# Feed-forward matmuls of 512 columns: high and low activations side by side

## The chip, the cores and the metric

The kernel runs on one core of a Trainium2 chip. The metric is the device time of one execution in microseconds (us). TensorE multiplies: a weight load (LDWEIGHTS) puts 128x128 values in its array, a MATMUL streams columns past them and adds the result into PSUM, which has eight banks of 512 float32 values on each of 128 partitions. VectorE and ScalarE read PSUM and do the elementwise work, GpSimd does a few small things, SyncE issues the weight DMAs.

## The reference

Two transformer blocks for 256 tokens of width 1024, in float32. The first has feed forward, a mixer, feed forward and a per-layer gate; the second has a mixer, memory attention and feed forward. Only the three feed-forward stages are touched by the change:

```python
def swiglu(x, w_gate, w_up, w_down):
    return (jax.nn.silu(x @ w_gate) * (x @ w_up)) @ w_down
...
        f = swiglu(rms_norm(h, ffn1_pre_g[i]), ffn1_w_gate[i], ffn1_w_up[i], ffn1_w_down[i])
        h = h + 0.5 * rms_norm(f, ffn1_post_g[i])
...
        gate, up = jnp.split(hf @ w_ffn_in[l], 2, axis=-1)
        x = x + (jax.nn.silu(gate) * up) @ w_ffn_out[l]
    return rms_norm_2(x, norm_final)
```

The width inside is 2816, which is 22 chunks of 128; the width outside is 8 chunks.

## The kernel before

Features lie on partitions, the 256 tokens on the free dimension. To get float32 accuracy out of the fast type float32r, each operand is split in two: a high part (a cast) and a low part (the rest, a subtraction). A product is then three matmuls, written in `mm3` (L187 to L190): high weights with high activations, low weights with high activations, high weights with low activations. Every `mm` is one weight load and one matmul at L184.

Weights come as blocks [128, 128], eight of them in a unit of 512 KB, in the order in which TensorE takes them. `Stream.take` hands out a block and sees to what is ahead of it: SyncE's DMA into a `raw` buffer (five of them), ScalarE's cast to the high part `wh` (L90, seven buffers, five units ahead) and VectorE's subtraction for the low part `wl` (L101, six buffers, four units ahead).

The order of all instructions is written by hand: each engine runs its own in the order in which the code issues them. Small steps are put off with `after(n, fn)`, and each `tick()` lets one more stretch of work pass.

`ffn` (called three times) has two parts.

- Gate and up: for the first four chunks of 128 outputs all eight input chunks are walked together, in four PSUM banks. Chunks 4 to 21 come one by one: `proj` runs 8 blocks for the gate into one half of a bank and 8 for the up branch into the other, so one unit of weights is one half chunk. Then `evac` multiplies the bank by 1/rms (`z`, L414, VectorE), applies Silu (L415, ScalarE), and puts off the product (s1, L418, VectorE), the high part `aH` (s2, L421, ScalarE) and the low part `aL` (s3, L424, VectorE) by one, two and three ticks.
- Down: for each of 8 output chunks, 22 blocks run into one half of a bank. `on_chunk` takes it away: in stages one and two `post_chunk` (a square, L304, a scaled copy, L330, both on ScalarE, and an addition, L305, on VectorE), in stage three `last_chunk` (an addition to the stream, L1223, on VectorE, then the rest).

The `pm` pool has five PSUM banks for these products, `pa` three for the rest. The activations' parts are separate tiles: `xH`, `xL` [128, 8, 256] and `aH`, `aL` [128, 22, 256]. While stage one runs, eight chunks of the memory operand are prepared by `mem_prep_chunk` (L464 to L467).

The mixers' `first_group` makes the values with tokens on partitions. There the activations are the loaded operand and four blocks of weights are streamed, so its matmuls have 512 columns.

Of the kernel before, what the change touches and what calls it, by code (L numbers as in the profile page):

```python
# [49 lines left out]
class Stream:  # L50
    """Weight blocks [128, 128] in the order in which the tensor engine takes them."""
# [19 lines left out]
    def split_now(self, u, cuts=(UB,)):  # L71
        """Both parts of unit u, for the start, when nothing else is to be done."""
# [43 lines left out]
def columns(a):  # L116
    """A view of 256 tokens in the order of the grid's columns as one in the order of its rows."""
    return a.rearrange("p (c r) -> p r c", r=GR)


class Bank:
    def __init__(self, t):
        self.t = t
        self.started = False


class Net:
# [63 lines left out]

    def mm3t(self, b, out, x, w, stop=False):
        self.mm(b, out, x[0], w[0])
        self.mm(b, out, x[0], w[1])
        self.mm(b, out, x[1], w[0], stop=stop)

    def proj(self, b, sub, name, m, ks, x):
        """One chunk of 128 outputs, features on partitions."""
        for i, k in enumerate(ks):
            w = self.ws.take(name, k, m)  # L200
            self.mm3(b, b.t[:, sub], w, (x[0][:, k], x[1][:, k]), stop=i == len(ks) - 1)
# [5 lines left out]
    def setup(self):  # L207
# [3 lines left out]
        self.xH = b.tile([P, DC, T], F32R, name="xH")  # L211
        self.xL = b.tile([P, DC, T], F32R, name="xL")
# [54 lines left out]
    def bcast(self, r):  # L267
        """1 / rms on every partition, in PSUM."""
# [28 lines left out]
    def squares(self, acc, in_, first, scale=1.0):  # L297
        """acc += (scale * in_)^2, chunk by chunk."""
# [8 lines left out]
    def sq_pair(self, j):  # L307
        """Squares of the stream's chunks 2j and 2j + 1."""
# [15 lines left out]
    def post_chunk(self, c, src, gain, scale=1.0):  # L324
        """Chunk c of a branch that is normed before it joins the stream."""
        nc = self.nc
        if c == 0:
            self.acc = self.new_acc()
        self.squares(self.acc, src, c == 0, scale)
        nc.scalar.activation(out=self.fg[:, c], in_=src, func=AF.Copy, scale=gain(c))  # L330

    def join(self, gain, fills, scale=None):
        """h += normed branch; then the next norm's operands, chunk by chunk."""
# [7 lines left out]
        x = (self.xH, self.xL)  # L341
# [43 lines left out]
    def add_chunk(self, c, src, gain, x):  # L385
        """h += branch, with the next norm's operands."""
# [7 lines left out]
    def add_pair(self, j, src, gain, x):  # L394
        """h += branch for two chunks of one bank, with the next norm's operands."""
# [8 lines left out]
    def ffn(self, gate, up, down, on_chunk, nk=4):  # L404
        nc = self.nc
        x = (self.xH, self.xL)
        with self.tc.tile_pool(name="ffn", bufs=1, reuse_waits="tile") as fp:
            self.fp = fp
            aH = fp.tile([P, FC, T], F32R, name="aH")
            aL = fp.tile([P, FC, T], F32R, name="aL")  # L410

            def evac(m, b):
                z = fp.tile([P, 2, T], F32, tag="z", name="z", bufs=6)
                nc.vector.tensor_tensor(out=z, in0=b.t, in1=self.row(rs), op=ALU.mult)  # L414
# [16 lines left out]
            for k in range(DC):  # L431
                for m in range(nk):
                    for sub, (name, off) in enumerate((gate, up)):
                        w = self.ws.take(name, k, off + m)
                        self.mm3(bs[m], bs[m].t[:, sub], w, (x[0][:, k], x[1][:, k]), stop=k == DC - 1)
# [4 lines left out]
            for m in range(nk):  # L440
                evac(m, bs[m])
            for m in range(nk, FC):
                b = self.bank()
                for sub, (name, off) in enumerate((gate, up)):
                    self.proj(b, sub, name, off + m, range(DC), x)
                    if sub == 1:
                        evac(m, b)
                    self.tick()
            for c in range(DC):
                b = self.bank()  # L450
                for k in range(FC):
                    w = self.ws.take(down, k, c)
                    self.mm3(b, b.t[:, 0], w, (aH[:, k], aL[:, k]), stop=k == FC - 1)
                    if k % 8 == 4:
                        self.tick()
                on_chunk(c, b.t[:, 0])

# [21 lines left out]
    def mem_k_task(self, c):  # L479
        nc = self.nc  # L480
        b = self.bank()
        for k in range(DC):
            w = self.ws.take("w_mem_kv_2", k, c)
            self.mm3(b, b.t[:, 0], w, (self.mH[:, k], self.mL[:, k]), stop=k == DC - 1)
# [29 lines left out]
    def ple_task(self, j):  # L514
        nc = self.nc
        b = self.bank()
        for sub in range(2):
            for k in range(2):
                w = self.ws.take("ple_w_proj", k, 2 * j + sub)
                self.mm3(b, b.t[:, sub], w, (self.pH[:, k], self.pL[:, k]), stop=k == 1)  # L520
# [6 lines left out]
    def first_group(self, win, vc, qc, kc):  # L527
        """Values (tokens on partitions) and the first two chunks of queries and keys, input chunk by chunk."""
        x = (self.xH, self.xL)
        vb = [self.bank() for _ in range(2)]  # L530
        qb = [self.bank() for _ in range(2)]
        for k in range(DC):
# [5 lines left out]
            for i in range(2):  # L538
                for sub, off in enumerate((qc, kc)):
                    w = self.ws.take(win, k, off + i)  # L540
                    self.mm3(qb[i], qb[i].t[:, sub], w, (x[0][:, k], x[1][:, k]), stop=k == DC - 1)
# [6 lines left out]
    def pair_task(self, win, m0, m1, evac):  # L548
        """Two output chunks in one bank; a generator of half tasks."""
        x = (self.xH, self.xL)  # L550
# [17 lines left out]
    def clear_pads(self, qz, vz):  # L568
        """The halves of queries and values that belong to a pair's other head."""
# [25 lines left out]
    def merge(self, tile, na, nb, oa, ob, tg, x, tanh_now):  # L595
        """merged = sigmoid(ga) * branch a + sigmoid(gb) * branch b, split, into x."""
# [25 lines left out]
    def from_merged(self, name, m, on_chunk):  # L622
        bs = [self.bank() for _ in range(2)]
        for ks in (range(DC - 2), (DC - 2, DC - 1)):
            for c in range(4):
                for k in ks:
                    w = self.ws.take(name, k, c)
                    self.mm3(bs[c // 2], bs[c // 2].t[:, c % 2], w, (m[0][:, k], m[1][:, k]), stop=k == DC - 1)
# [13 lines left out]
    def mixer1(self, fills):  # L642
        nc, tc, d = self.nc, self.tc, self.d
        with tc.tile_pool(name="mix1", bufs=1, reuse_waits="tile") as mp:
# [9 lines left out]
            oH = mp.tile([P, 4, T], F32R, name="oH")  # L654
            oL = mp.tile([P, 4, T], F32R, name="oL")
            yH = mp.tile([P, 4, T], F32R, name="yH")
            yL = mp.tile([P, 4, T], F32R, name="yL")
# [78 lines left out]
            def pool_mm(g):  # L736
                b = self.flat_bank()
                w = self.ws.take("pool_w", g, 0)
                self.mm3(b, b.t[:, 0:T], w, (yH[:, g], yL[:, g]), stop=True)
# [82 lines left out]
            m = (self.xH, self.xL)  # L822
# [589 lines left out]
```

## Time and profile before

| | |
|---|---|
| time, median of 3 runs | 1041.7 us (1041.17 to 1041.95) |
| span of the profiled execution, first to last instruction | 1040.2 us |
| TensorE busy | 1030.7 us, 99% |
| VectorE busy | 709.6 us, 68% |
| ScalarE busy | 545.7 us, 52% |
| GpSimd busy | 44.0 us, 4% |
| matmuls recorded | 8606 |

A profile is one execution; each record has a start and a length, and PE is TensorE's matmuls, PEld its weight loads, DVE VectorE, ACT ScalarE. Records of matmuls overlap, since the next one starts before the last one's results are all in PSUM, and a matmul's end is modelled. The distance between two starts tells what one costs in a row.

### The profile page before, as it was taken

Reading aid. Unit: us, or ns where it says so; the run is one execution under the profiler, and the core shown is the slowest. Engines: PE = TensorE matmul, PEld = TensorE weight load, DVE = VectorE, ACT = ScalarE, POOL = GpSimd, SP = SyncE. Lnnn points to the kernel's source line nnn. Section 1 sums busy time; section 2 is a strip of 40 time slices with the busy share of each in tenths; the row PEclk is TensorE's granted clock in tenths of the full one; section 3 lists DMA queues with packets and bytes.
Section 4 is the critical chain, followed back from the end, with each engine's and each line's share of the span. In section 5 each row is a group of like instructions: output and inputs, shape, how many; then the busy total and the mean of one; then the engine's idle time right before and its main releaser. Section 6 shows DMA issues by size and latency. Waiting matters only on the chain.

```text
span 1040.2 us, 20720 instructions
## 1 busy us (share of the span) xinstructions
PE 1030.7 (99%) x8606; PEld 1022.6 (98%) x8606; DVE 709.6 (68%) x1062; ACT 545.7 (52%) x857; POOL 44.0 (4%) x73
## 2 busy tenths in 40 slices
PE   9999999999999999999999999999999999999997
PEld 8999999999999999999999999999999999999996
DVE  7777754587858677666447776886678677666642
ACT  7655544464644555454446565465556555544431
POOL 0100000120000110000000111000001000000000
PEclk9999999999999999999999999999999999999999
DMA  8765564555545655556555666454566346555541
GB/s 287 244 214 181 194 215 171 181 190 185 194 151 166 229 179 193 184 191 190 196 167 177 195 201 194 159 168 157 160 222 226 110 139 219 187 199 182 178 147 42
DMA packets 55023, 191.50 MB, mean 184 GB/s; under 512 B 6400, under 2 KB 7936, under 8 KB 54928
## 3 DMA queue, kind: packets, MB, share of 16 engines
q1 hardware_dynamic: 52992, 184.37, 53.6%
q0 software_dynamic: 1936, 5.80, 1.8%
q8 instruction: 67, 1.10, 0.4%
q14 instruction: 28, 0.23, 0.1%
HBM read 187.00 MB, written 3.15 MB: 183 GB/s over the span
## 4 chain that ended last, share of the span: by engine, by line
PE 81%; issue 16%; DMA 1%; DVE 1%; SPq 0%; POOL 0%; POOLq 0%; DVEq 0%; ACT 0%
PE mm L184 77%; PE at L184 3%; DMA raw<-ws 1%; PE at L839 1%; DMA hg<-gx 0%; DVE sqp L315 0%; POOL r L264 0%; DVE wl L79 0%; SPq L63 0%; DVE wl L101 0%; DVE xL L290 0%; DVE fg L1323 0%; POOLq L1405 0%; DVEq L1405 0%; ACT wh L78 0%
## 5 line engine op out<-in xcount | busy, mean ns | idle before, releaser
L184 PE MATMUL mm<-xH,wh 128*128 128x256 f32 x1760 | 494.9, 281 | 0.0
L184 PE MATMUL mm<-xH,wl 128*128 128x256 f32 x1760 | 492.2, 280 | 0.8 <-DVE wl L79 0.4
L184 PE MATMUL mm<-xL,wh 128*128 128x256 f32 x1760 | 491.4, 279 | 0.0
L101 DVE TENSOR_TENSOR wl<-raw,wh 128x1024 fp32r<-128x1024 f32 x340 | 405.8, 1218 | 22.0 <-ACT wh L90 7.4
L90 ACT CAST wh<-raw 128x1024 fp32r<-128x1024 f32 x340 | 350.2, 1046 | 53.0 <-PE mm L184 33.5
L184 PEld LDWEIGHTS mm<-xH,wl 128*128 128x128 f32 x1760 | 331.2, 188 | 2.6 <-DVE wl L79 1.4
L184 PEld LDWEIGHTS mm<-xH,wh 128*128 128x128 f32 x1760 | 331.3, 188 | 1.6 <-ACT wh L78 0.8
L184 PEld LDWEIGHTS mm<-xL,wh 128*128 128x128 f32 x1760 | 331.1, 188 | 0.0
L184 PE MATMUL mm<-aH,wh 128*128 128x256 f32 x528 | 148.9, 282 | 0.0
L184 PE MATMUL mm<-aL,wh 128*128 128x256 f32 x528 | 148.2, 281 | 0.0
L184 PE MATMUL mm<-aH,wl 128*128 128x256 f32 x528 | 148.2, 281 | 0.0
L415 ACT ACTIVATE z<-z 128x256 f32<-128x256 f32 x66 | 27.2, 418 | 145.6 <-DVE z L414 145.5
L184 PEld LDWEIGHTS mm<-aH,wl 128*128 128x128 f32 x528 | 99.6, 189 | 0.0
L184 PEld LDWEIGHTS mm<-aH,wh 128*128 128x128 f32 x528 | 99.6, 189 | 0.0
L184 PEld LDWEIGHTS mm<-aL,wh 128*128 128x128 f32 x528 | 99.5, 189 | 0.0
L414 DVE TENSOR_TENSOR z<-mm,rs 128x512 f32<-128x512 f32 x66 | 44.7, 689 | 77.5 <-PE mm L184 71.8
L305 DVE TENSOR_TENSOR acc<-acc,sq 128x256 f32<-128x256 f32 x27 | 11.5, 425 | 65.0 <-ACT sq L304 64.9
L264 POOL TENSOR_TENSOR r<-v,mhalf 128x2 f32<-128x2 f32 x13 | 17.6, 1355 | 685.7 <-DVE v L262 685.7
L286 ACT ACTIVATE xH<-hg 128x256 fp32r<-128x256 f32 x48 | 23.6, 543 | 31.9 <-DVE hg L355 22.0
L304 ACT ACTIVATE sq<-mm 128x256 f32<-128x256 f32 x21 | 8.2, 390 | 53.8 <-PE mm L184 53.8
L418 DVE TENSOR_TENSOR z<-z 128x256 f32<-128x256 f32 x66 | 27.2, 423 | 8.7 <-ACT z L415 7.5
L424 DVE TENSOR_TENSOR aL<-z,aH 128x256 fp32r<-128x256 f32 x66 | 26.6, 415 | 0.0
(238 smaller groups left out, 1225.9 us busy)
## 6 DMA issues: line engine op xcount, KB each, us to landing
raw<-ws SPq DMA_DIRECT2D x340, 512.0 KB, 4.1
raw<-ws SPq DMA_DIRECT2D x9, 256.0 KB, 6.0
ub<-ub SPq DMA_DIRECT2D x8, 160.0 KB, 2.9
mraw<-memT POOLq DMA_DIRECT2D x8, 128.0 KB, 3.7
kd<-kv POOLq DMA_DIRECT2D x8, 128.0 KB, 3.0
vd<-kv POOLq DMA_DIRECT2D x4, 256.0 KB, 3.4
kv<-kd POOLq DMA_DIRECT2D x4, 256.0 KB, 6.2
kv<-vd POOLq DMA_DIRECT2D x4, 256.0 KB, 7.1
```

The lines of the kernel that those rows point to most:

```text
L90: self.nc.scalar.copy(out=h, in_=self.R[self.nhigh])
L101: self.nc.vector.tensor_tensor(out=l, in0=self.R.pop(u), in1=self.H[u].bitcast(F32), op=ALU.subtract)
L184: self.nc.tensor.matmul(out, lhsT, rhs, start=not b.started, stop=stop, skip_group_check=True)
L264: nc.gpsimd.tensor_tensor(out=r, in0=v, in1=self.mhalf, op=ALU.pow)
L286: self.nc.scalar.activation(out=self.ordered(x[0][:, c]), in_=self.rows(self.h[:, c]), func=AF.Copy, scale=gain(c))
L304: nc.scalar.activation(out=s, in_=in_, func=AF.Square, scale=scale)
L305: nc.vector.tensor_tensor(out=acc, in0=acc, in1=s, op=ALU.add)
L414: nc.vector.tensor_tensor(out=z, in0=b.t, in1=self.row(rs), op=ALU.mult)
L415: nc.scalar.activation(out=z[:, 0], in_=z[:, 0], func=AF.Silu)
L418: nc.vector.tensor_tensor(out=z[:, 0], in0=z[:, 0], in1=z[:, 1], op=ALU.mult)
L424: nc.vector.tensor_tensor(out=aL[:, m], in0=z[:, 0], in1=aH[:, m].bitcast(F32), op=ALU.subtract)
L839: self.nc.tensor.transpose(b.t[:, i * T + t * P:i * T + (t + 1) * P], u[:, t, kt * P:(kt + 1) * P], self.ident)
```

## The change

In the three feed-forward stages the product of a block is written with two matmuls, by a new `mm2`: the high weights meet high and low activations in one matmul of 512 columns, which fills both halves of a bank, and the low weights meet the high activations in one of 256, which is added to the first half. The two halves are summed at eviction. So that 512 columns lie side by side, every pair of high and low tiles becomes one tile [128, chunks, 2, 256] (class `Split`), also outside the feed-forward stages, where only the way of naming the parts changes. The first four chunks of gate and up, the last chunk of down, and all other stages keep `mm3`.

```diff
+class Split:
+    def __getitem__(self, i):
+        return self.t[:, :, i]
+    def at(self, k):
+        return self.t[:, k, 0], self.t[:, k, 1], self.t[:, k]
...
+    def mm2(self, b, w, x, stop=False):
+        self.mm(b, b.t, w[0], x[2])
+        self.mm(b, b.t[:, 0], w[1], x[0], stop=stop)
+
+    def wide(self, b, name, m, ks, x):
+        for i, k in enumerate(ks):
+            self.mm2(b, self.ws.take(name, k, m), x.at(k), stop=i == len(ks) - 1)
...
-        self.xH = b.tile([P, DC, T], F32R, name="xH")
-        self.xL = b.tile([P, DC, T], F32R, name="xL")
+        self.x = Split(b.tile([P, DC, 2, T], F32R, name="x"))
...
+        if more is not None:
+            nc.scalar.copy(out=self.fg[:, c], in_=more)
+            nc.vector.tensor_tensor(out=self.fg[:, c], in0=src, in1=self.fg[:, c], op=ALU.add)
+            src = self.fg[:, c]
...
-            aH = fp.tile([P, FC, T], F32R, name="aH")
-            aL = fp.tile([P, FC, T], F32R, name="aL")
...
+            a = Split(fp.tile([P, FC, 2, T], F32R, name="a"))
+            aH, aL = a[0], a[1]
...
+            def join2(z, b):
+                nc.scalar.copy(out=z, in_=b.t[:, 1])
+                nc.vector.tensor_tensor(out=z, in0=b.t[:, 0], in1=z, op=ALU.add)
...
             for m in range(nk, FC):
-                b = self.bank()
+                z = zt()
                 for sub, (name, off) in enumerate((gate, up)):
-                    self.proj(b, sub, name, off + m, range(DC), x)
+                    b = self.bank()
+                    self.wide(b, name, off + m, range(DC), x)
+                    join2(z[:, sub], b)
                     if sub == 1:
-                        evac(m, b)
+                        evac(m, z, z)
                     self.tick()
             for c in range(DC):
                 b = self.bank()
+                two = c < DC - 1
                 for k in range(FC):
                     w = self.ws.take(down, k, c)
-                    self.mm3(b, b.t[:, 0], w, (aH[:, k], aL[:, k]), stop=k == FC - 1)
+                    if two:
+                        self.mm2(b, w, a.at(k), stop=k == FC - 1)
+                    else:
+                        self.mm3(b, b.t[:, 0], w, a.at(k), stop=k == FC - 1)
                     if k % 8 == 4:
                         self.tick()
-                on_chunk(c, b.t[:, 0])
+                on_chunk(c, b.t[:, 0], b.t[:, 1] if two else None)
...
         nc.vector.tensor_tensor(out=h[:, c], in0=src, in1=h[:, c], op=ALU.add)
+        if more is not None:
+            nc.vector.tensor_tensor(out=h[:, c], in0=more, in1=h[:, c], op=ALU.add)
```

What stands in a row on VectorE in the gate and up part of stage one, before. The number behind a name is that of the buffer, so `mm_680` is a bank; in square brackets are the semaphores that an instruction waits for.

```order
L101 TENSOR_TENSOR wl_685<-raw_537,wh_641 128x1024 [waits DMAHW5_49]
L101 TENSOR_TENSOR wl_716<-raw_572,wh_683 128x1024 [waits DMAHW6_49,Activation_49]
L414 TENSOR_TENSOR z_742<-mm_680,rs_446 128x512 [waits PE_49]
L424 TENSOR_TENSOR aL_189<-z_669,aH_188 128x256 [waits Activation_49]
L418 TENSOR_TENSOR z_742<-z_742 128x256 [waits Activation_49]
L101 TENSOR_TENSOR wl_752<-raw_608,wh_714 128x1024 [waits DMAHW7_49]
```

The same place on VectorE after the change.

```order
L101 TENSOR_TENSOR wl_650<-raw_524,wh_612 128x1024 [waits DMAHW5_49]
L443 TENSOR_TENSOR z_644<-mm_645,z_644 128x256 [waits Activation_49]
L101 TENSOR_TENSOR wl_676<-raw_554,wh_648 128x1024 [waits DMAHW6_49]
L443 TENSOR_TENSOR z_644<-mm_671,z_644 128x256 [waits Activation_49]
L446 TENSOR_TENSOR z_644<-z_644,rs_443 128x512 [waits DVE_49]
L456 TENSOR_TENSOR a_186<-z_582,a_186 128x256
L450 TENSOR_TENSOR z_644<-z_644 128x256 [waits Activation_49]
L101 TENSOR_TENSOR wl_706<-raw_584,wh_674 128x1024 [waits DMAHW7_49]
```

Two additions (L443) have come in, one after each half chunk, and the first of them stands between two weight splits that followed each other before; the z multiplication reads the sum and no longer the bank.

ScalarE at the same place, before:

```order
L421 CAST aH_188<-z_528 128x256 [waits DVE_49]
L90 CAST wh_574<-raw_464 128x1024 [waits DMAHW3_49,PE_49,Activation_49]
L415 ACTIVATE z_602<-z_602 128x256 [waits DVE_49]
L90 CAST wh_610<-raw_498 128x1024 [waits DMAHW4_49,PE_49,Activation_49]
L421 CAST aH_188<-z_602 128x256 [waits DVE_49]
L90 CAST wh_641<-raw_537 128x1024 [waits DMAHW5_49,PE_49,Activation_49]
```

And after:

```order
L90 CAST wh_648<-raw_554 128x1024 [waits DMAHW6_49]
L442 COPY z_644<-mm_645 128x256 [waits PE_49,Activation_49]
L453 CAST a_186<-z_582 128x256 [waits DVE_49]
L90 CAST wh_674<-raw_584 128x1024 [waits DMAHW7_49]
L442 COPY z_644<-mm_671 128x256 [waits PE_49]
L447 ACTIVATE z_644<-z_644 128x256 [waits DVE_49]
L90 CAST wh_704<-raw_610 128x1024 [waits DMAHW0_49]
```

A copy out of the bank (L442) that waits for TensorE now stands behind each weight cast.

## Rows read from the trace of the kernel before

**Rows 1.** The page, part 1: busy time, share, instructions of each engine.

```profile
PE 1030.7 (99%) x8606; PEld 1022.6 (98%) x8606; DVE 709.6 (68%) x1062; ACT 545.7 (52%) x857; POOL 44.0 (4%) x73
```

**Rows 2.** The cores: span and mean granted TensorE clock.

```profile
core 0: 1040.2 us, clock 0.998
```

**Rows 3.** TensorE's waits: who waited for whom, total us, times, longest us.

```profile
PE at L230 <- DVE fg L227: 1.2, 1, 1.2
PE at L184 <- ACT sq L1235: 1.0, 1, 1.0
PE mm L184 <- DVE wl L79: 0.4, 2, 0.2
PE mm L184 <- DVE wl L101: 0.3, 1, 0.3
```

**Rows 4.** Groups by shape: line, engine, out<-in, shape, count | busy us, mean ns | idle.

```profile
L184 PE MATMUL mm<-xL,wh 128*128 128x256 f32 x1760 | 491.4, 279 | 0.0
L184 PE MATMUL mm<-wh,xL 128*128 128x512 f32 x32 | 12.7, 397 | 0.0
L184 PEld LDWEIGHTS mm<-xL,wh 128*128 128x128 f32 x1760 | 331.1, 188 | 0.0
```

**Rows 5.** Timeline of VectorE, gate and up, stage two: start us, length us [idle before].

```profile
431.73 0.69 DVE L414 TENSOR_TENSOR z<-mm,rs 128x512 f32<-128x512 f32 x1 [1.73 <-PE mm L184]
432.33 0.41 DVE L424 TENSOR_TENSOR aL<-z,aH 128x256 fp32r<-128x256 f32 x1
432.90 0.42 DVE L418 TENSOR_TENSOR z<-z 128x256 f32<-128x256 f32 x1 [0.16 <-ACT z L415]
433.25 2.35 DVE L101 TENSOR_TENSOR wl<-raw,wh 128x1024 fp32r<-128x1024 f32 x2
437.33 0.69 DVE L414 TENSOR_TENSOR z<-mm,rs 128x512 f32<-128x512 f32 x1 [1.73 <-PE mm L184]
```

**Rows 6.** Timeline of TensorE in the first mixer's first group: start us, length us.

```profile
207.05 0.40 PE L184 MATMUL mm<-wh,xH 128*128 128x512 f32 x1
...
208.21 0.40 PE L184 MATMUL mm<-wh,xL 128*128 128x512 f32 x1
208.45 0.28 PE L184 MATMUL mm<-xH,wh 128*128 128x256 f32 x1
...
209.85 0.39 PE L184 MATMUL mm<-wh,xH 128*128 128x512 f32 x1
...
221.05 0.39 PE L184 MATMUL mm<-wh,xH 128*128 128x512 f32 x1
```

**Rows 7.** Groups by shape: an addition out of PSUM, a copy out of PSUM.

```profile
L1223 DVE TENSOR_TENSOR hg<-mm,hg 128x256 f32<-128x256 f32 x8 | 3.4, 425 | 31.8 <-PE mm L184 31.8
L276 ACT COPY rs<-at 128x256 f32<-128x256 f32 x6 | 2.2, 372 | 17.4 <-PE at L184 17.4
```

**Rows 8.** Timeline of VectorE in stage one, a pair with memory preparation.

```profile
64.28 0.69 DVE L414 TENSOR_TENSOR z<-mm,rs 128x512 f32<-128x512 f32 x1 [1.73 <-PE mm L184]
65.86 0.48 DVE L466 SCALAR_TENSOR_TENSOR mL<-mraw,hg,mH 128x256 fp32r<-128x256 f32 x1 [0.89 <-ACT mH L465]
...
69.88 0.69 DVE L414 TENSOR_TENSOR z<-mm,rs 128x512 f32<-128x512 f32 x1 [0.26 <-PE mm L184]
```

**Rows 9.** Timeline at the end: the last product and its addition.

```profile
1031.46 0.29 PE L184 MATMUL mm<-aL,wh 128*128 128x256 f32 x1
1031.79 0.42 DVE L1223 TENSOR_TENSOR hg<-mm,hg 128x256 f32<-128x256 f32 x1 [7.12 <-PE mm L184]
```

**Rows 10.** Timeline of TensorE: first matmul of down in stage one, first after it.

```profile
132.17 0.28 PE L184 MATMUL mm<-aH,wh 128*128 128x256 f32 x1
...
194.83 0.28 PE L184 MATMUL mm<-mH,wh 128*128 128x256 f32 x1
```

**Rows 11.** Timeline of TensorE: first mixer's branch products and what follows them.

```profile
308.61 0.28 PE L184 MATMUL mm<-yH,wl 128*128 128x256 f32 x1
...
331.53 0.28 PE L184 MATMUL mm<-xH,wh 128*128 128x256 f32 x1
```

More of the change, by code (lines that the diff above doesn't have):

```diff
@@ L200, in proj @@
             w = self.ws.take(name, k, m)
-            self.mm3(b, b.t[:, sub], w, (x[0][:, k], x[1][:, k]), stop=i == len(ks) - 1)
+            self.mm3(b, b.t[:, sub], w, x.at(k), stop=i == len(ks) - 1)
     def row(self, t):
@@ L322, in new_acc, with post_chunk @@
         return self.tmp.tile([P, T], F32, tag="acc", name="acc", bufs=2)
-    def post_chunk(self, c, src, gain, scale=1.0):
+    def post_chunk(self, c, src, gain, scale=1.0, more=None):
         nc = self.nc
@@ L483, in mem_k_task @@
             w = self.ws.take("w_mem_kv_2", k, c)
-            self.mm3(b, b.t[:, 0], w, (self.mH[:, k], self.mL[:, k]), stop=k == DC - 1)
+            self.mm3(b, b.t[:, 0], w, self.m.at(k), stop=k == DC - 1)
             if k < DC - 1:
@@ L519, in ple_task @@
                 w = self.ws.take("ple_w_proj", k, 2 * j + sub)
-                self.mm3(b, b.t[:, sub], w, (self.pH[:, k], self.pL[:, k]), stop=k == 1)
+                self.mm3(b, b.t[:, sub], w, self.p.at(k), stop=k == 1)
                 if 2 * sub + k < 3:
@@ L540, in first_group @@
                     w = self.ws.take(win, k, off + i)
-                    self.mm3(qb[i], qb[i].t[:, sub], w, (x[0][:, k], x[1][:, k]), stop=k == DC - 1)
+                    self.mm3(qb[i], qb[i].t[:, sub], w, x.at(k), stop=k == DC - 1)
             if k == DC - 2:
@@ L653, in mixer1 @@
             tg2 = mp.tile([P, 4, 2, T], F32, name="tg2")
[L654 to L657, printed above, removed]
+            o = Split(mp.tile([P, 4, 2, T], F32R, name="o"))
+            y = Split(mp.tile([P, 4, 2, T], F32R, name="y"))
+            oH, oL, yH, yL = o[0], o[1], y[0], y[1]
             tg1 = self.fg.rearrange("p (a b) t -> p a b t", b=2)
@@ L738, in pool_mm @@
                 w = self.ws.take("pool_w", g, 0)
-                self.mm3(b, b.t[:, 0:T], w, (yH[:, g], yL[:, g]), stop=True)
+                self.mm3(b, b.t[:, 0:T], w, y.at(g), stop=True)
                 sc = self.gv[:, G_SCALE + g:G_SCALE + g + 1]
@@ L1151, in trans @@
                 b = self.transposed(st[h])
-                pH, pL = (mp.tile([P, 2, T], F32R, tag="p" + i, name="p" + i, bufs=n) for i, n in (("H", 2), ("L", 1)))
+                p = Split(mp.tile([P, 2, 2, T], F32R, tag="p", name="p", bufs=2))
+                pH, pL = p[0], p[1]
                 bt = b.t.rearrange("p (a t) -> p a t", a=2)
@@ L1217, in memory, with last_chunk @@
             outk((6, 7), True)
-    def last_chunk(self, c, src):
+    def last_chunk(self, c, src, more):
         nc = self.nc
```

79 lines of the change are left out of this document (41 added, 38 removed).

## The prediction

> **What bounds the kernel now.** The page's busy shares come first [rows 1]: TensorE has work in 99% of the span, VectorE in 68%, ScalarE in 52%. The view of the cores [rows 2] gives a mean granted clock of 0.998, so TensorE stands at its 2.4 GHz level nearly all the time. The view of TensorE's waits comes next [rows 3]: it waited 1.2 us for the set-up, 1.0 us at the very end and 0.7 us for weight parts in 1040.2 us. So no engine feeds TensorE too slowly, and the time is the sum of what its instructions cost in a row. An edit can gain only by making those cheaper, and can lose by making them dearer or by letting something late enough to stop them.
>
> A busy share does not say what one instruction costs. The groups by shape [rows 4] give 280 ns for a matmul of 256 columns, about 400 ns for one of 512 and 188 ns for a weight load, but the records overlap, so these are lengths and not prices. The price is the distance from start to start. In the gate and up part VectorE's evictions mark it: the start of one z multiplication to the next is 437.33 - 431.73 = 5.60 us [rows 5], and between them TensorE runs 2 x 8 blocks of three matmuls, 48 in all. That is 116.7 ns for 256 columns, or 350 ns for a block. The clock alone would allow 256/2.4 = 106.7 ns. The question is whether the missing 10 ns belong to the instruction or to the columns.
>
> **The change on TensorE.** Each block of weights used three matmuls of 256 columns (high x high, low x high, high x low). Now it uses one of 512 (high weights against both parts of the activations) and one of 256. The columns stay 768; one matmul and one weight load go. Counting from the loops: 18 chunks x 2 x 8 = 288 blocks in the gate and up part, 7 x 22 = 154 in the down part, three feed-forward stages, so 3 x 442 = 1326 instructions go.
>
> Their price can be read in the first mixer, where the values are already made by matmuls of 512 columns [rows 6]. One step there is six matmuls of 512 and twelve of 256, 18 instructions and 6144 columns. Five steps take 221.05 - 207.05 = 14.00 us, 2.800 us each. Twenty-four matmuls of 256, the same columns in 24 instructions, take 24 x 116.7 = 2.800 us in the gate and up part. Six instructions fewer save nothing. Inside a step, six of 512 take 208.45 - 207.05 = 1.40 us and twelve of 256 take 209.85 - 208.45 = 1.40 us: the time goes with the columns, 0.456 ns each. The rows are good to 0.01 us; on 5.60 us that is 5 ns for 24 matmuls, so a fixed cost above 0.8 ns per instruction would show. TensorE's term is therefore 1326 x 0, within plus or minus 1326 x 0.8 ns = 1.1 us. I take 0, the middle, because the two quotients are equal.
>
> The Trainium skill says otherwise: "TensorE: Matmul & The Clock Gate", section "Back-to-back issue gap", gives N/2.4 + 2.5 ns from start to start, so a fixed 2.5 ns per matmul; by it the sum would be 1326 x 2.5 = 3.3 us less, an estimate. Its 109 ns for 256 columns and 216 for 512 are below the 116.7 and 233 of these rows, and the step of 2.800 us does not show its fixed part. The page "Perfetto Trace Analysis", section "Identifying the Most-Contended Engine", judges TensorE by the busy share of its weight loads, which here is 98% of the span; taken at its word it speaks for the change, which takes a third of the loads away in these stages. The rows differ: with one load for 512 columns the pace is what it is with one load for 256.
>
> **The change on the evictions.** The two sums of a block chain now stand in the two halves of a bank. In gate and up each half chunk gets a ScalarE copy of one half and a VectorE addition of the other, 36 of each per stage. In down the first seven chunks of stages one and two get the same pair, and those of stage three one more addition. None of these existed; the nearest rows are an addition out of PSUM of this shape, 425 ns, and a ScalarE copy out of PSUM, 372 ns [rows 7]. For the whole kernel that is 129 additions more on VectorE (55 us) and 122 copies on ScalarE (45 us), all beside TensorE as long as it never waits for them.
>
> Does it? The pair of half chunks shown is the test. In 5.60 us VectorE now runs z, the low part aL, the product, and two weight splits from 431.73 to 435.60, and then idles 1.73 us until TensorE has finished the next pair [rows 5]. After the change two additions (0.85 us) come in, and once a pair VectorE stands for the ScalarE copy that its addition needs (0.4 us). 1.73 - 0.85 - 0.4 leaves about 0.5 us idle: VectorE still ends ahead of TensorE. The order also moves one of the two weight splits behind the other half chunk's addition, so it now waits for TensorE's first half chunk; it splits a unit needed four units (11.2 us) later, so nobody notices 2.8 us. In stage one eight pairs also carry the memory's preparation: there the waits are 0.89 and 0.26 us [rows 8], 1.15 us against 1.25 us of new work, a pair that ends 0.1 us late, and the next pair has 0.5 us to catch up. ScalarE's queue gets two copies (0.75 us) between weight casts that have a lead of five units; what is queued behind a waiting copy is the next cast, and it has 14 us.
>
> A bank now holds half a chunk, not a whole one, and is free only after the addition, some 0.8 us after its last matmul. TensorE takes a new bank every 2.8 us and five rotate, so a bank is wanted again some 11 us after it was finished. In down a matmul now needs both parts of an activation chunk at its start; the last low part is issued at block 12 of the first 22 and wanted at block 21, 9 x 0.35 = 3.1 us later, with one split (1.2 us) and itself (0.4 us) to do. Cost 0; without that cover it would be at most 1 us in each stage. The last chunk of down keeps the old form, so the tail after the final matmul (1031.46 to the end [rows 9]) and the two joins start as before: 0.
>
> **The sum.** 0 on TensorE (-1.1 to +1.1), 0 on the evictions, 0 at the seams: a span of 1040.2 us again. The runs had a median of 1041.7, 1.5 us above that span, which does not change: I forecast **1041.5**, between 1040.4 and 1043.
>
> **Rivals.**
> (A) There is a fixed cost per matmul after all, which shows when 512 and 256 alternate at every instruction. The before trace alternates only in runs of six and twelve. For it: 10 ns per matmul are unexplained by the clock. Against it: the step of 2.800 us includes a change each way. At three times the resolution of the rows, 2.4 ns, it gives 1326 x 2.4 ns = 3.2 us: **1038.5**. Chance 0.12. The rule of "TensorE: Matmul & The Clock Gate" in the Trainium skill would end there too.
> (B) The down part speeds up. From the first matmul on a to the first that follows it, 528 take 194.83 - 132.17 = 62.66 us [rows 10], 118.7 ns each and not 116.7. If that extra 2 ns comes from where the high and low parts lie or from the weight loads, it may go: 462 blocks x 3 x 2 ns = 2.8 us, **1038.9**. Against it: a keeps its place and size, only the parts are interleaved. Chance 0.13; with some other gain, 0.02.
> (C) The slower side: the pace depends on which tile is streamed, and the re-laid tiles fall on a slow one. The mixer's branch products stream other tiles, and 191 matmuls there take 331.53 - 308.61 = 22.92 us [rows 11], 120.0 ns each at the same clock. If every merged block went at this pace, gate and up would lose 864 x 3 x 3.3 ns = 8.6 us and down 462 x 3 x 1.3 ns = 1.8 us: **1052**. If gate and up only fell to the pace of down, 864 x 3 x 2 ns = 5.2 us, **1046.7**. It decides from 0.5 ns per 256 columns on. Against it: x is at 116.7 in this stage and keeps its place. Chance 0.05 for the full price, 0.07 for the smaller.
> (D) VectorE becomes the bound in gate and up. It needs more than 5.60 us of work in a pair, 0.5 us over my count. At 1 us over, 18 pairs fall 18 us behind, 11 of them covered by the lead: 7 us in each stage, **1062**. Chance 0.03.
>
> **How the numbers follow.** The forecast has 0.58; A 0.12, B 0.13, other gains 0.02; C 0.12; D 0.03. A measurement here tells about 0.2% (2.1 us) from no change, so faster 0.27, same 0.58, slower 0.15. The range 1037.8 to 1047 leaves out A and B together, the full C and D, some 0.15.
>
> **What would show it.** Right: z to z in gate and up again about 5.60 us, starts 0.233 and 0.117 us apart in alternation; TensorE's matmul count down by 1326 and its share still 99%; VectorE idle some 0.5 us in a pair. A: a pair of 512 and 256 below 0.348 us. B: the down part of a stage below 61.8 us. C: a pair above 0.352 us in gate and up. D: TensorE waiting for the wl splits or for the L443 additions. I would be wrong if one merged pair differs from 0.350 us by more than 2 ns.

## The result, and the profile after

The changed kernel takes 1034.9 us (median, 1034.7 to 1035.3); the kernel before, measured beside it, 1041.8 us (1041.2 to 1042.5). The ratio is 0.9935, 95% interval 0.9921 to 0.9949: 7 us faster, below the forecast of 1040.4 to 1043 and below its wider range from 1037.8 on. The span fell from 1040.2 to 1032.9 us at the same mean granted clock, 0.998.

The page's first part, busy time of each engine (beside [rows 1]):

```profile
PE 1023.2 (99%) x7280; PEld 961.8 (93%) x7280; DVE 758.4 (73%) x1191; ACT 585.2 (57%) x979; POOL 44.0 (4%) x73
```

8606 - 7280 = 1326 matmuls are gone, as counted; VectorE and ScalarE have the new work (129 and 122 instructions more). TensorE is at 99% as before, so the gain is not idle time that was filled. TensorE's waits say the same (who waited for whom, total us, times, longest us); they are those of [rows 3] within 0.1 us:

```profile
PE at L252 <- DVE fg L249: 1.2, 1, 1.2
PE at L197 <- ACT sq L1275: 1.0, 1, 1.0
PE mm L197 <- DVE wl L101: 0.4, 1, 0.4
PE mm L197 <- DVE wl L79: 0.4, 2, 0.2
```

So the matmuls themselves became cheaper. Where, the starts at the borders of the feed-forward stages tell. Timeline of TensorE in the changed kernel, first matmul of down and first matmul after it in stages one and two, first and last of down in stage three (start us, length us):

```profile
130.97 0.40 PE L197 MATMUL mm<-a,wh 128*128 128x512 f32 x1
...
192.11 0.28 PE L197 MATMUL mm<-m,wh 128*128 128x256 f32 x1
...
483.87 0.40 PE L197 MATMUL mm<-a,wh 128*128 128x512 f32 x1
...
545.01 0.28 PE L197 MATMUL mm<-p,wh 128*128 128x256 f32 x1
...
961.10 0.40 PE L197 MATMUL mm<-a,wh 128*128 128x512 f32 x1
...
1024.16 0.28 PE L197 MATMUL mm<-a,wh 128*128 128x256 f32 x1
```

In the kernel before, those of stage one are [rows 10], the last is in [rows 9], and the other three are these:

```profile
487.52 0.28 PE L184 MATMUL mm<-aH,wh 128*128 128x256 f32 x1
...
550.18 0.28 PE L184 MATMUL mm<-pH,wh 128*128 128x256 f32 x1
...
967.24 0.28 PE L184 MATMUL mm<-aH,wh 128*128 128x256 f32 x1
```

| stretch | before, us | after, us | gained, us |
|---|---|---|---|
| start to the end of gate and up, stage one | 132.17 | 130.97 | 1.20 |
| down, stage one | 62.66 | 61.14 | 1.52 |
| to the end of gate and up, stage two | 292.69 | 291.76 | 0.93 |
| down, stage two | 62.66 | 61.14 | 1.52 |
| to the end of gate and up, stage three | 417.06 | 416.09 | 0.97 |
| down, stage three | 64.22 | 63.06 | 1.16 |

Down gained 4.2 us and the rest 3.1 us, of the 7.3 us of the span. Each stretch that holds 288 merged blocks of gate and up is about 1 us shorter. The mixers and the memory attention, where nothing was merged, gave nothing that shows.

What one merged pair costs is read in gate and up, stage two. Timeline of TensorE:

```profile
431.17 0.39 PE L197 MATMUL mm<-x,wh 128*128 128x512 f32 x1
431.40 0.28 PE L197 MATMUL mm<-x,wl 128*128 128x256 f32 x1
431.52 0.39 PE L197 MATMUL mm<-x,wh 128*128 128x512 f32 x1
...
433.25 0.39 PE L197 MATMUL mm<-x,wh 128*128 128x512 f32 x1
```

From 431.17 to 433.25 there are six pairs: 2.08 us, 346.7 ns each, where three matmuls of 256 took 350.0. In down of stages one and two the mean of 176 blocks is 347.4 ns (61.14 us / 176), with the 22 blocks of the last chunk in it, which kept three matmuls; the merged pairs alone go at 346.7 ns there too, where three matmuls took 356.0 (62.66 us / 176 blocks). 864 x 3.3 ns = 2.9 us in gate and up and the 4.2 us of down make 7.1 of the 7.3 us; the rest lies in stage one, whose 1.20 us are more than 288 x 3.3 ns = 0.96 us.

VectorE in one pair of half chunks of the same stage, beside [rows 5] (start us, length us [idle before]):

```profile
429.46 0.69 DVE L446 TENSOR_TENSOR z<-z,rs 128x512 f32<-128x512 f32 x1
430.07 0.42 DVE L456 TENSOR_TENSOR a<-z,a 128x256 fp32r<-128x256 f32 x1
430.64 0.43 DVE L450 TENSOR_TENSOR z<-z 128x256 f32<-128x256 f32 x1 [0.15 <-ACT z L447]
430.98 1.22 DVE L101 TENSOR_TENSOR wl<-raw,wh 128x1024 fp32r<-128x1024 f32 x1
432.12 0.42 DVE L443 TENSOR_TENSOR z<-mm,z 128x256 f32<-128x256 f32 x1
432.45 1.22 DVE L101 TENSOR_TENSOR wl<-raw,wh 128x1024 fp32r<-128x1024 f32 x1
434.55 0.42 DVE L443 TENSOR_TENSOR z<-mm,z 128x256 f32<-128x256 f32 x1 [0.88 <-ACT z L442]
435.01 0.69 DVE L446 TENSOR_TENSOR z<-z,rs 128x512 f32<-128x512 f32 x1
```

z to z is 435.01 - 429.46 = 5.55 us, against 5.60. The two additions L443 are there, and VectorE still stands for 0.88 us until TensorE has finished the next half chunk and ScalarE has copied it.

### The profile page after: what moved, and what is told of

Read it like the earlier page. It is cut to its first block, busy times and chain, and to the rows that moved or that the text cites. A ratio compares the mean times of both kernels' runs of the same rounds, so it can differ in the third digit from the quotient of the medians.

```text
span 1032.9 us, 18212 instructions
## 1 busy us (share of the span) xinstructions
PE 1023.2 (99%) x7280; PEld 961.8 (93%) x7280; DVE 758.4 (73%) x1191; ACT 585.2 (57%) x979; POOL 44.0 (4%) x73
## 4 chain that ended last, share of the span: by engine, by line
PE 81%; issue 16%; DMA 1%; DVE 1%; SPq 0%; POOL 0%; POOLq 0%; DVEq 0%; ACT 0%
PE mm L197 77%; PE at L197 3%; DMA raw<-ws 1%; PE at L876 1%; DMA hg<-gx 0%; DVE sqp L337 0%; POOL r L286 0%; DVE wl L79 0%; SPq L63 0%; DVE wl L101 0%; DVE x L312 0%; DVE fg L1363 0%; POOLq L1445 0%; DVEq L1445 0%; ACT wh L78 0%
## 5 line engine op out<-in xcount | busy, mean ns | idle before, releaser
L197 PE MATMUL mm<-x,wh 128*128 128x256 f32 (+1 forms) x2784 | 650.3, 315 | 0.1
L197 PE MATMUL mm<-x,wl 128*128 128x256 f32 x1824 | 512.3, 281 | 0.9 <-DVE wl L101 0.4
L197 PEld LDWEIGHTS mm<-x,wh 128*128 128x128 f32 x2784 | 459.5, 188 | 35.5 <-ACT wh L78 1.0
L197 PEld LDWEIGHTS mm<-x,wl 128*128 128x128 f32 x1824 | 343.8, 189 | 2.7 <-DVE wl L79 1.2
L197 PE MATMUL mm<-a,wh 128*128 128x512 f32 (+1 forms) x594 | 185.2, 368 | 0.0
L197 PE MATMUL mm<-a,wl 128*128 128x256 f32 x528 | 147.5, 280 | 0.0
L197 PEld LDWEIGHTS mm<-a,wh 128*128 128x128 f32 x594 | 107.2, 188 | 19.1
L197 PEld LDWEIGHTS mm<-a,wl 128*128 128x128 f32 x528 | 99.2, 188 | 0.0
L443 DVE TENSOR_TENSOR z<-mm,z 128x256 f32<-128x256 f32 x108 | 45.3, 420 | 30.0 <-ACT z L442 29.8
L442 ACT COPY z<-mm 128x256 f32<-128x256 f32 x108 | 39.5, 366 | 33.0 <-PE mm L197 32.7
```

What stands on the lines that cost most here:

```text
L197: self.nc.tensor.matmul(out, lhsT, rhs, start=not b.started, stop=stop, skip_group_check=True)
L442: nc.scalar.copy(out=z, in_=b.t[:, 1])
L443: nc.vector.tensor_tensor(out=z, in0=b.t[:, 0], in1=z, op=ALU.add)
```

## The experiments

Two theories stood at first. One: the columns are now side by side and the streaming of the re-laid tiles is what got cheaper. The other: fewer matmuls, at some fixed cost of each. The first four kernels do one part of the change each.

**The new tiles alone.** All tiles as in the changed kernel, all products by three matmuls of 256.

```diff
-                    b = self.bank()
-                    self.wide(b, name, off + m, range(DC), x)
-                    join2(z[:, sub], b)
+                    self.proj(b, sub, name, off + m, range(DC), x)
...
-                two = c < DC - 1
+                two = False
```

> The changed kernel with all its interleaved tiles, but every product again by three matmuls of 256 columns and the old evictions. Theory: a matmul with its weight load costs 17/16 cycle of the 2.4 GHz clock per column and 8 cycles (3.3 ns) by itself, so the gain comes from the removed matmuls, and interleaving alone helps only in down, where the last chunk, which kept three matmuls, went from 118.7 to about 117.3 ns: gate and up 350 ns a block as before, down 352, time about 1040. Rival, the place of the tiles gives the whole gain: gate and up 346.7 ns a block or less, time about 1035.

Timeline of TensorE in gate and up, six blocks apart (rows merged by kind):

```profile
431.02 0.40 PE L197 MATMUL mm<-x,wh 128*128 128x256 f32 x2
...
433.12 0.40 PE L197 MATMUL mm<-x,wh 128*128 128x256 f32 x2
```

Measured: 1042.2 us, ratio to before 1.001 (1.0001 to 1.0019), span 1040.1. Gate and up stay at 2.10 us / 6 = 350.0 ns per block. The tiles give nothing.

**Merged, but the parts apart.** The changed kernel with high and low parts again in two halves of a tile, so that the 512 columns are two stretches.

```diff
-        return self.t[:, k, 0], self.t[:, k, 1], self.t[:, k]
+        return self.t[:, 0, k], self.t[:, 1, k], self.t[:, :, k]
...
-            a = Split(fp.tile([P, FC, 2, T], F32R, name="a"))
+            a = Split(fp.tile([P, 2, FC, T], F32R, name="a"))
```

> The changed kernel with its matmuls of 512 columns, but the high parts of all chunks lie together and the low parts behind them, as far apart as before; the 512 columns are two runs of 256. Theory, the removed matmul counts: gate and up 346.7 ns a block as in the changed kernel, down 347 to 352, time 1035 to 1037. Rival, interleaving counts: 350 and 356 ns a block as before, time about 1041.8.

Timeline of TensorE in gate and up, six pairs apart:

```profile
431.04 0.39 PE L197 MATMUL mm<-x,wh 128*128 128x512 f32 x1
...
433.12 0.39 PE L197 MATMUL mm<-x,wh 128*128 128x512 f32 x1
```

Measured: 1035.3 us, 0.9941 (0.9928 to 0.9953); over whole stretches a pair takes 346.7 ns in gate and up and in down, as in the changed kernel. The whole gain belongs to the merged matmuls; side by side they need not lie.

**Merged in one part of a stage only.** First gate and up alone (`two = False` in down), then down alone (`proj` in gate and up).

> The changed kernel with the merged matmuls in gate and up only; down by three matmuls from the interleaved tile. Theory: 864 removed matmuls at 3.3 ns give 2.9 us, the layout in down some 1.5 to 2 us: about 1037.3. Rival, the place of the tiles gives everything: about 1035.

> The changed kernel with the merged matmuls in down only; gate and up by three matmuls and the old evictions. Theory: what gate and up gained is lost, 2.9 us over the changed kernel, about 1037.8; down 346.7 ns a block. Rival, the place of the tiles gives everything: about 1035.

Measured: 1040.8 us, 0.9995 (0.9986 to 1.0003), and 1037.4 us, 0.9963 (0.9949 to 0.9976). Down alone gives its 4 us. Gate and up alone seem to give nothing, though their pairs take 346.7 ns there too. The timeline of TensorE, from one execution, shows where some of it went: first matmul of down in stage one and first one after it, in the kernel with gate and up merged:

```profile
130.54 0.28 PE L197 MATMUL mm<-a,wh 128*128 128x256 f32 x1
...
193.90 0.28 PE L197 MATMUL mm<-m,wh 128*128 128x256 f32 x1
```

63.36 us for 176 blocks is 360.0 ns, where the kernel before has 356.0 [rows 10]. In the kernel with the new tiles alone, where down has the same instructions and operands, it runs at 356.0 in stage one and at 352.0 in stage two. So an untouched stretch took back 0.7 us in each of stages one and two (in stage three down takes 64.22 us, as before). Three matmuls of 256 have no fixed price. Over all runs, such blocks of the feed-forward stages go at 350, 352, 356 or 360 ns, steadily through a whole stretch.

Stage three shows it inside the kernel before. There transposes cut down into pieces of 22 blocks. Timeline of TensorE, starts of the second and of the last block of two such pieces:

```profile
988.25 0.28 PE L184 MATMUL mm<-aH,wh 128*128 128x256 f32 x1
...
995.29 0.28 PE L184 MATMUL mm<-aH,wh 128*128 128x256 f32 x1
...
1004.20 0.28 PE L184 MATMUL mm<-aH,wh 128*128 128x256 f32 x1
...
1011.32 0.28 PE L184 MATMUL mm<-aH,wh 128*128 128x256 f32 x1
```

Twenty blocks take 7.04 us in the first, 352.0 ns each, and 7.12 us in the second, 356.0 ns. A piece of the changed kernel:

```profile
981.67 0.39 PE L197 MATMUL mm<-a,wh 128*128 128x512 f32 x1
...
988.60 0.39 PE L197 MATMUL mm<-a,wh 128*128 128x512 f32 x1
```

Twenty merged pairs take 6.93 us, 346.5 ns each. In every traced kernel that has them in turn, merged pairs of gate and up and of down go at 346.7 ns, within 0.3 ns, once a stretch is past its first blocks.

**A break before down.** If that pace is set where a stretch begins, a single matmul of one column (two records in the trace) between gate and up and down may shift it. The kernel before, plus:

```diff
+            pause = self.abank()
+            nc.tensor.matmul(pause.t[:, 0:1], self.ident, self.ones, start=True, stop=True)
             for c in range(DC):
```

> The kernel before with one tiny matmul of 1 column, whose result nobody reads, ahead of the down part of each feed-forward stage. The down part ran at 356.0 ns a block before, and at 352.0 and 360.0 in stages of the first four experiments with the same operands, at the same pace from its first matmuls to its last. Theory: three matmuls of 256 fall into one of several steady rhythms, and which one is set at the entry; a break at the entry changes it, so down leaves 356.0 (350 would give 1040.0, 360 1043). Rival, the pace belongs to the tile a: 356.0 in stages one and two, time 1041.5.

Timeline of TensorE, the break, the first matmul of down and the first one after it:

```profile
131.36 0.28 PE L450 MATMUL at<-ones,ident 128*128 128x1 f32 x2
131.50 0.37 PE L184 MATMUL mm<-aH,wh 128*128 128x256 f32 x1
...
193.54 0.28 PE L184 MATMUL mm<-mH,wh 128*128 128x256 f32 x1
```

62.04 us with the restart in it; after that, blocks go at 352.0 ns instead of 356.0, to the end of the stretch. The time, 1040.8 us, ratio 0.9991 (0.9982 to 1.0001), can hardly tell this from no change, but the starts can: extra work made the same matmuls quicker. So some 4 of the 9.3 ns that merging gave in down (356.0 to 346.7) belong to the pace that this stretch happened to have, not to the price of the matmuls that went.

**Another order of the three.** The kernel before with high x high, high x low, low x high, so that one set of weights is loaded twice running.

```diff
         self.mm(b, out, w[0], x[0])
-        self.mm(b, out, w[1], x[0])
-        self.mm(b, out, w[0], x[1], stop=stop)
+        self.mm(b, out, w[0], x[1])
+        self.mm(b, out, w[1], x[0], stop=stop)
```

> The kernel before with the three matmuls of a block in another order: high weights with high activations, high weights with low activations, low weights with high activations. All loads and matmuls stay; only the change of weights between the first two is gone. Theory, the matmul with its load is what costs: gate and up 350 ns a block, time 1039 to 1043. Rival, changing from high to low weights and back costs, and merging saved one of these changes: gate and up 346.7 ns a block, time about 1038 or less.

Measured: 1041.1 us, 0.9995 (0.9986 to 1.0005); gate and up at 350.0 ns. Which weights follow which plays no part there.

**Matmuls of 128 columns.** The kernel before with each matmul of gate and up's chunks 4 to 21 cut in two; twice the weight loads, the same columns.

```diff
-                    self.proj(b, sub, name, off + m, range(DC), x)
+                    for k in range(DC):
+                        w = self.ws.take(name, k, off + m)
+                        for hh in range(2):
+                            s = slice(hh * P, hh * P + P)
+                            self.mm3(b, b.t[:, sub, s], w, (x[0][:, k, s], x[1][:, k, s]), stop=k == DC - 1)
```

> The kernel before with the opposite edit: chunks 4 to 21 of gate and up by six matmuls of 128 columns a block instead of three of 256, the same columns and the same evictions. Theory, every matmul with its load costs 8 cycles (3.3 ns) beside 17/16 cycle a column: three more per block cost 10 ns, 350 becomes 360, 864 blocks give 8.6 us, time about 1050. Rival, the reading on which the prediction stood (only columns cost): 350 ns a block, time 1041.5.

Measured: 1318.6 us, 1.2663 (1.2644 to 1.2682), far above what was expected. Timeline of TensorE, thirteen matmuls apart:

```profile
61.00 0.28 PE L184 MATMUL mm<-xH,wh 128*128 128x128 f32 x1
...
62.45 0.27 PE L184 MATMUL mm<-xH,wl 128*128 128x128 f32 x1
```

1.45 us / 13 is 111.5 ns (111.7 over the stretch) for half of the columns that take 116.7 ns. A matmul with a weight load of its own does not get below that here, and 256 columns stand 5 ns above this floor. That the weight load sets the floor is likely, but not shown. Above the floor taking loads away saves no load time: the run with 512 columns alone, below, has half as many loads for its columns and the same price per column.

**The control that the prediction lacked.** It had compared a step of the first mixer, with values made by matmuls of 512, with 256s in another stage. Here the same step is made of 256s alone.

```diff
-                self.mm3t(vb[t], vb[t].t.rearrange("p a b -> p (a b)"), (x[0][:, k, s], x[1][:, k, s]), w,
-                          stop=k == DC - 1)
+                for hh in range(2):
+                    self.mm3t(vb[t], vb[t].t[:, hh], (x[0][:, k, s], x[1][:, k, s]),
+                              [e[:, hh * T:(hh + 1) * T] for e in w], stop=k == DC - 1)
```

> The kernel before with the matmuls of 512 columns of the mixers' first group cut in two of 256, so that a step has 24 matmuls, not 18. Reading of the prediction, only columns cost: 2.800 us a step as before. Theory: these matmuls stream weights from the weight buffers, at a rhythm of their own (120 ns per 256 where the memory's values are made), and the equality with 24 matmuls of x was a coincidence: 12 x 120 + 12 x 116.7 = 2.840 us a step.

Timeline of TensorE, start of the first step, of its part behind the values, of the second and of the sixth step:

```profile
206.96 0.28 PE L184 MATMUL mm<-wh,xH 128*128 128x256 f32 x1
...
208.38 0.28 PE L184 MATMUL mm<-xH,wh 128*128 128x256 f32 x1
...
209.79 0.28 PE L184 MATMUL mm<-wh,xH 128*128 128x256 f32 x1
...
221.11 0.28 PE L184 MATMUL mm<-wh,xH 128*128 128x256 f32 x1
```

In this single run (1042.4 us) five steps take 221.11 - 206.96 = 14.15 us, 2.830 each, against 2.800 for the same five in [rows 6]: six matmuls more cost 30 ns, 5.0 ns each. By this row the forecast would have been 1326 x 5.0 = 6.6 us below before.

**Without the additions at eviction.** The changed kernel leaving out the second sum in gate and up (36 VectorE additions in each stage).

```diff
-                nc.scalar.copy(out=z, in_=b.t[:, 1])
-                nc.vector.tensor_tensor(out=z, in0=b.t[:, 0], in1=z, op=ALU.add)
+                nc.scalar.copy(out=z, in_=b.t[:, 0])
```

> The changed kernel without the 108 additions on VectorE in gate and up: ScalarE copies the first half of the bank and the second half (high weights with low activations) is left out of the sum. Theory: the evictions are hidden behind TensorE, whose pace stays at 346.7 ns a block: the time of the changed kernel, about 1034.9, within 0.5. Rival, VectorE's added work eats part of the gain: 1 us or more below the changed kernel, 1034 or less.

Measured: 1035.1 us, 0.9937 (0.9925 to 0.995), the same as with them: they lie beside TensorE entirely.

**512 columns alone.** The changed kernel without the matmuls of the low weights in gate and up, to see what 512 columns cost with no 256 among them.

```diff
-            self.mm2(b, self.ws.take(name, k, m), x.at(k), stop=i == len(ks) - 1)
+            w = self.ws.take(name, k, m)
+            self.mm(b, b.t, w[0], x.at(k)[2], stop=i == len(ks) - 1)
```

> The changed kernel with gate and up (chunks 4 to 21) reduced to the matmul of 512 columns: the low weights' matmul of 256 is left out. It shows what 512 columns of activations cost one after the other, where the load of the next weights has 213 ns to hide. The trace of matmuls of 128 columns showed 111 ns from start to start, so there the weight load sets the pace, and at 256 columns 116.7 is close to it. Theory, a fixed cost on top of 17/16 cycle a column: 230.0 ns each. Reading of the prediction, only columns, at 0.456 ns: 233.3 ns each. Rival, the load is the whole excess over the clock and vanishes behind 512 columns: 213 to 216 ns each.

Timeline of TensorE, 55 matmuls apart (rows merged by kind):

```profile
377.92 0.63 PE L197 MATMUL mm<-x,wh 128*128 128x512 f32 x2
...
390.76 0.63 PE L197 MATMUL mm<-x,wh 128*128 128x512 f32 x2
```

Measured, in a single run: 1004.0 us. The 55 matmuls take 12.84 us; over the 744 distances between starts that are below 260 ns, so have no wait in them, the mean is 233.3 ns: 0.456 ns per column, as for 256 alone. A fixed cost per matmul would have put it below. The columns left out are worth 864 x 116.7 ns = 101 us; the time is only 31 us below the changed kernel's, because now VectorE is too slow. The first of TensorE's waits:

```profile
PE mm L197 <- DVE z L444: 28.8, 35, 2.0
```

That leaves a puzzle. 512 alone take 233.3, 256 alone 116.7, together 350.0; in turn they take 346.7. Either the removed matmul saves after all when a 256 follows, or the taking turns does. The next two kernels keep every instruction of the changed one and only regroup gate and up: eight 512s and then eight 256s, or two and two.

```diff
-        for i, k in enumerate(ks):
-            self.mm2(b, self.ws.take(name, k, m), x.at(k), stop=i == len(ks) - 1)
+        for g in range(0, len(ks), 8):
+            ws = [(k, self.ws.take(name, k, m)) for k in ks[g:g + 8]]
+            for k, w in ws:
+                self.mm(b, b.t, w[0], x.at(k)[2])
+            for k, w in ws:
+                self.mm(b, b.t[:, 0], w[1], x.at(k)[0], stop=k == ks[-1])
```

> The changed kernel with the matmuls of gate and up regrouped: for each half chunk first eight matmuls of 512 columns (high weights), then eight of 256 columns (low weights), instead of one of each in turn. Same instructions and same sums; only the order in which the two widths follow one another differs. Alone on their row, 512 columns took 233.3 ns each (the run with the matmuls of 512 alone) and 256 columns 116.7 ns (the kernel before), together 350.0; in turn they take 346.7. Theory 'alternation' (the 3.3 ns come from a wide and a narrow matmul taking turns): gate and up go back to 350.0 ns per pair, 864 pairs lose 2.9 us, the time is 1037.7 us. Rival 'one matmul less' (the saving belongs to the removed matmul and its weight load, in whatever order the others come): 346.7 ns per pair on average, 1034.9 us.

> The same with groups of two: two matmuls of 512 columns, then two of 256. Theory 'alternation', a gain for each change of width: half as many changes as in the changed kernel, so half of the 3.3 ns, 348.3 ns per pair and 1036.3 us. Rival 'one matmul less': 346.7 ns per pair, 1034.9 us.

Timeline of TensorE with groups of eight (rows merged by kind; start us, length us, count):

```profile
429.98 2.03 PE L197 MATMUL mm<-x,wh 128*128 128x512 f32 x8
431.84 1.11 PE L197 MATMUL mm<-x,wl 128*128 128x256 f32 x8
432.78 2.03 PE L197 MATMUL mm<-x,wh 128*128 128x512 f32 x8
```

and with groups of two:

```profile
430.81 0.62 PE L197 MATMUL mm<-x,wh 128*128 128x512 f32 x2
431.27 0.40 PE L197 MATMUL mm<-x,wl 128*128 128x256 f32 x2
...
432.89 0.62 PE L197 MATMUL mm<-x,wh 128*128 128x512 f32 x2
```

In eights, 432.78 - 429.98 = 2.80 us for eight pairs, 350 ns (350.8 over stages one and two, 350.0 in stage three): the saving in gate and up is gone, and the time is 1038.4 us, 0.9967 (0.9955 to 0.998), 3.5 us above the changed kernel. In twos, 432.89 - 430.81 = 2.08 us for six pairs, 346.7 ns as in turn, 1035.0 us, 0.9935 (0.9921 to 0.995). The number of matmuls is the same in all three, so removing a matmul is not by itself what saves. Nor does each change of width save something, since half as many changes save as much. Short groups of both widths go at 346.7 ns, long runs of one width at 350. Inside the twos the mean distance after a 512 is 227.7 ns and after a 256 118.9 ns; in the eights 233.4 and 117.5: the wide ones gain 5.7 ns, the narrow ones lose 1.4 (means over some 230 starts of each width in stage two). What in TensorE does this stays open, and so does the group size at which it ends.

**A version meant to beat both.** The changed kernel with the mixers' pairs of chunks merged as well, in `pair_task`:

```diff
-        self.proj(b, 0, win, m0, range(DC), x)
...
+        z = Bank(self.tmp.tile([P, 2, T], F32, tag="sqp", name="sqp", bufs=3))
+        for sub, m in enumerate((m0, m1)):
+            b = self.bank()
+            self.wide(b, win, m, range(DC), x)
+            self.nc.scalar.copy(out=z.t[:, sub], in_=b.t[:, 1])
+            self.nc.vector.tensor_tensor(out=z.t[:, sub], in0=b.t[:, 0], in1=z.t[:, sub], op=ALU.add)
```

> The changed kernel with the same merge also in the two mixers' projections that come in pairs of chunks: 28 pairs of 16 blocks, 448 more matmuls removed, 56 more copies and additions. Theory: 448 x 3.3 ns = 1.5 us, about 1033.4, if VectorE, which is busier there, keeps ahead. Rival, VectorE or the banks, which the scores share there, stop TensorE: 1035 or more.

Measured: 1040.3 us, 0.9988 (0.9979 to 0.9998), so 5.4 us slower than the changed kernel. TensorE's waits have a new first row:

```profile
PE at L878 <- DVE u L871: 4.6, 5, 1.4
```

In the mixers VectorE also does the softmax (`u`, L871), and transposes on TensorE (L878) wait for it. The additions that feed-forward hides come on the path there. All five waits lie in the first mixer: from the end of down in stage one to down in stage two this kernel takes 297.5 us, 5.7 us more than the changed one, while from there to stage three it takes 0.5 us less (415.6 against 416.1).

## Why the prediction was wrong

**What bounds the kernel.** Right: the waits did not change, TensorE stayed at 99%, and the whole difference is in the distance from start to start.

**The count.** Right: 1326 matmuls.

**TensorE's term, 1326 x 0.** This step failed, mis-sized by the whole result: it measured 2.9 us in gate and up and 4.2 us in down. That the time goes with the columns, 0.456 ns each, holds, within the spread of the paces, where many matmuls of one width follow one another: 512 alone cost 233.3 ns, and groups of eight cost 350.0 to 350.8 ns a pair. What failed is carrying this over from the runs of six and twelve in [rows 6] to matmuls of two widths in turn, which cost 346.7 ns a pair. For that the prediction took two equal quotients, 2.800 us for a step of the mixer and 2.800 us for 24 matmuls in another stage, as proof that an instruction costs nothing, and even gave the bound as 0.8 ns. The quotients were equal by chance: the pace of one shape differs from stretch to stretch by up to 3%, more than what was asked. Three matmuls of 256 took 350.0 to 360.0 ns, and the 356.0 and 360.0 stood in [rows 10] and [rows 11]. The same step with 256s alone takes 2.830 us. A comparison within one stretch would have given 5.0 ns per matmul, 1035.1 us, near the result, though in part by luck: the groups of eight show that no fixed price goes with a matmul. The bound should have been the spread of the same shape in these rows, about 3 ns per 256 columns, and not the resolution of a start.

**The evictions.** Right: no wait of TensorE on them, and leaving the additions out changes nothing. VectorE's slack came out as estimated: 0.5 us idle plus 0.4 us for the copy were forecast at the pair's end, and 0.88 us is there.

**The seams.** Right: the tail from the last matmul of down to the span's end is 1032.9 - 1024.2 = 8.7 us, as before (1040.2 - 1031.5).

**Rival A, a fixed cost that shows when 512 and 256 alternate.** Its mark, a pair below 348 ns, is there, and 3.3 ns per removed matmul in gate and up are near its 2.4. Its condition, alternation at every instruction, was nearly the right one too (groups of two do as well). Its mechanism was not: 512 alone cost 233.3, and in groups of eight the same matmuls save nothing. The Trainium skill's formula in "TensorE: Matmul & The Clock Gate", section "Back-to-back issue gap", which the section gives for an isolated matmul, ends near by luck as well: its 2.5 ns would be saved in whatever order the matmuls come, and the run with groups of eight shows none of it.

**Rival B, down speeds up.** It came true too (61.14 us, its mark was 61.8), and for more than its 2.8 us (4.2). The extra 2 ns per matmul were neither of the tile nor of the weight loads: a one-column matmul ahead of the stretch removed part of them, with both as they were, and with gate and up alone merged they were more.

**Rival C, the pace belongs to the tile.** Right that it varies by that much, wrong on what it hangs. The slow pace never met merged blocks; where it came, in down of the kernel with gate and up alone merged, it took back 1.4 of their 2.9 us.

**Rival D, VectorE as the bound.** Not here, but it is near: it decided the kernel with 512 alone and the one with the mixers merged.

**The chances.** A and B were treated as excluding each other, and the range left out "A and B together". They are two stretches with the same doubt, the price of a 256 in a row, so they should have been given as one case. Together they made 1035.7 us, which is near the result.

The second page cited, "Perfetto Trace Analysis" of the Trainium skill, section "Identifying the Most-Contended Engine", judges TensorE by its weight loads' busy share, beside the share of the peak that its arithmetic reaches. That busy share fell from 98% to 93% and the time by 0.7%, so it pointed the right way; the size is not in it, and 512 columns with one load cost as much as twice 256 with one each (233.3 ns), so from 256 columns on the loads do not set the pace.

## What to carry to other kernels

When a saving per instruction is smaller than the spread of one shape's pace between stretches, two stretches can't be compared to price it: make the row and its control in the same stretch, and use the spread as the bound. A local edit can also move the pace of an untouched stretch behind it, so read the starts stretch by stretch before a total is taken as the edit's worth. And work added at eviction is free only where the evicting engine has slack: count it anew in every stage.

## What was not expected of the hardware

- With a weight load for each, a matmul of 128 columns starts 111.7 ns after the last one, one of 256 116.7 ns: going from 256 to 128 columns saves almost nothing.
- The same stretch of matmuls of 256 runs at one of several steady paces (350, 352, 356, 360 ns for three) at a mean granted clock of 0.997 to 0.998, and the pace is kept until something interrupts it. What picks it stays open.
- Groups of one or two matmuls of 512 and of 256 columns in turn go 1% quicker than groups of eight or one width alone (346.7 against 350.0 to 350.8 ns for 768 columns).
